# Weight operand buffers begun 16 to 128 bytes further, or hi and lo matmuls in another order, one variant for each MLP quarter

## The chip, the cores and the metric

The kernel runs on one core of one Trainium2 chip. The metric is the time of one execution in microseconds (us) of device time; lower is better. Times are given as the median of several runs. A profile comes from one further execution, whose instructions are recorded one by one.

## What is computed

A two-layer encoder trunk on 256 tokens of width 2048, in float32. Each layer mixes tokens with three groups of attention heads, and then runs an MLP whose hidden width is 8192. Cut to what the change touches:

```python
for l in range(DEPTH):                                   # DEPTH = 2
    ...                                                  # projections, attention, w_out
    u = jnp.square(jax.nn.relu(_rms(x, ln2_g[l]) @ w_ff1[l]))   # (256, 2048) @ (2048, 8192)
    x = x + u @ w_ff2[l]                                        # (256, 8192) @ (8192, 2048)
return _rms(x, ln_f_g)
```

## The kernel before

**Work as a row of units.** Every weight matrix is cut into units of at most 128 x 2048 values, which are listed in one order by hand (`layer_units`). The kernel walks this list. For unit i it writes the matmuls of TensorE, then the loads and splits of later units, then the evacuation of the unit's result. All five engines follow the written order; semaphores alone decide when each instruction may start.

**From a unit to operands.** SyncE's queue loads a unit into one of three `raw` buffers (L132). `split_to` then cuts it into chunks of 1024 columns. ScalarE rounds a chunk into a `hi` buffer (L147), VectorE subtracts and writes the rest into a `lo` buffer (L148). `hi` and `lo` have five buffers each, of 1024 values (4096 bytes) in a partition. Together they hold a float32 weight in two parts of type fp32r. Activations are kept in the same way, with the high part in columns 0 to 255 of a tile and the low part in columns 256 to 511 (`hx` for the inputs of a layer half, `ring` for others).

**The MLP.** In each layer it runs in four quarters of the hidden width. In each quarter 16 units named f come first and 16 named g after them. Quarter (l, q) below is quarter q of layer l, both counted from 0.

- An f unit makes 128 hidden columns. `mm_tile` runs over 16 k-tiles. For each it writes two matmuls into one PSUM bank, `acc`. The first, "h" here, has the hi weight tile (128 x 128) standing in the array and streams the 512 columns of `hx` (high and low part). The second, "l" here, has the lo weight tile standing and streams only the 256 columns of the high part into columns 256 to 511 of the bank. The two rows L297 and L298 of the profile are h and l. The first f unit of a layer has its own copy of this loop (L904, L905), with work between the k-tiles.
- A g unit multiplies back. In `v_mm` the activations stand in the array and the weights stream, 512 columns in each matmul: three matmuls (L616 to L618) for each k-tile and half of the tokens.

Each matmul has a weight load of its own (LDWEIGHTS, engine PEld in the profile), which the compiled program places ahead of it.

**The ring of small tiles.** `t1k` hands out tiles `t` of 128 x 256 from six buffers. The evacuation of an f unit takes two: one for the copied second half (L252), one for the sum (L253), which is then squared and split (L915 to L918). The first projections of a layer hold up to four `t` tiles, which GpSimd squares (L200 to L204).

**Addresses.** In the program as built, every `hi` and `lo` buffer, every `hx` tile and every `ring` tile begins on a multiple of 64 bytes in its partition. `hi`, `lo` buffers lie 4096 bytes apart before the change.

Of the kernel before, what the change touches and what calls it, by code (L numbers as in the profile page):

```python
# [10 lines left out]
F32 = mybir.dt.float32  # L11
F32R = mybir.dt.float32r
# [5 lines left out]
P = 128  # L18
T = 256
# [5 lines left out]
HL_BUFS = 5  # L25
# [14 lines left out]
def layer_units():  # L40
    names = [f"s{c}" for c in range(4)] + [f"a{m}" for m in range(4, 8)]
    names += ["b0", "b1", "un", "b2", "b3", "ur", "b4", "b5", "uk", "b6", "b7", "uv"]
    names += [f"v{k}" for k in range(8)]
    names += [f"c{m}" for m in range(12)]
    names += [f"o{m}" for m in range(10)]
    names += [f"w{m}" for m in range(6)]
    names += [f"p{m}" for m in range(8)]
    for q in range(4):
        names += [f"f{16 * q + m}" for m in range(16)]
        names += [f"g{16 * q + m}" for m in range(16)]  # L50
    cols = {"ur": 1024, "o": 1024, "w": 1024}
    return [(n, cols.get(n, cols.get(n[0], 2048))) for n in names]


UNITS = layer_units()
POS = {n: i for i, (n, _) in enumerate(UNITS)}


@with_exitstack
def kernel(  # L60
# [11 lines left out]
    pe, act, dve, pool, sp = nc.tensor, nc.scalar, nc.vector, nc.gpsimd, nc.sync  # L72
# [3 lines left out]
    sb = ctx.enter_context(tc.tile_pool(name="sb", bufs=1))  # L76
# [4 lines left out]
    def nm(s):  # L81
        uid[0] += 1
        return f"{s}_{uid[0]}"
# [5 lines left out]
        return sb.tile([P, 512], F32R, tag="hx", name=nm("hx"), bufs=16)  # L89

    def t1k():
        return sb.tile([P, T], F32, tag="t", name=nm("t"), bufs=6)

    def z2():
        return sb.tile([P, 512], F32, tag="z2", name=nm("z2"), bufs=4)
# [4 lines left out]
    def accbank():  # L100
        return ps.tile([P, 512], F32, tag="acc", name=nm("acc"), bufs=4)
# [3 lines left out]

    units = [(l,) + u for l in range(DEPTH) for u in UNITS]
    chunks = []
# [26 lines left out]
    def load_to(u):  # L134
        while loaded[0] < min(u, len(units)):
            load_part(loaded[0], 0, unit_src[loaded[0]][2])
            loaded[0] += 1

    def split_to(c):
        while splitted[0] < min(c, len(chunks)):  # L140
            k = splitted[0]
            u, o, n = chunks[k]
            load_to(u + 1)
            t = raw_t[u][:, o:o + n]
            hi = sb.tile([P, 1024], F32R, tag="hi", name=nm("hi"), bufs=HL_BUFS)
            lo = sb.tile([P, 1024], F32R, tag="lo", name=nm("lo"), bufs=HL_BUFS)
            act.activation(out=hi[:, :n], in_=t, func=AF.Copy)  # L147
            dve.tensor_tensor(out=lo[:, :n], in0=t, in1=hi[:, :n].bitcast(F32), op=ALU.subtract)  # L148
            hi_t[k], lo_t[k] = hi, lo
            splitted[0] += 1  # L150
            if k == unit_chunks[u][-1]:
                load_to(u + 1 + RAW_BUFS)
# [97 lines left out]
    def zevac(acc, dst):  # L250
        t = t1k()
        act.activation(out=t, in_=acc[:, T:], func=AF.Copy)  # L252
        dve.tensor_tensor(out=dst, in0=acc[:, :T], in1=t, op=ALU.add)  # L253
# [30 lines left out]
    def wtile(i, t, w=P):  # L284
        o = t * w
        for c in unit_chunks[i]:
            n = chunks[c][2]
            if o < n:
                return hi_t[c][:, o:o + w], lo_t[c][:, o:o + w]
            o -= n  # L290

    def mm_tile(i, t0, srcs, acc):
        n = len(srcs)
        for k in range(n):
            h, lo = wtile(i, t0 + k)
            s = srcs[k]
            pe.matmul(acc, h, s, start=k == 0, stop=False)  # L297
            pe.matmul(acc[:, T:], lo, s[:, :T], start=False, stop=k == n - 1)  # L298

    def layer(l):  # L300
# [3 lines left out]
        def at(name, pos, f, d=0):  # L304
            i = POS[name] if isinstance(name, str) else name
            sched[base + i + d, pos].append(f)

        def define(name, f, e):
            slot_pe[base + POS[name]], slot_ev[base + POS[name]] = f, e

# [35 lines left out]
        def gemm_acc(name, t0, srcs, acc=None):  # L346
            if acc is None:
                acc = accbank()
            mm_tile(base + POS[name], t0, srcs, acc)
            return acc  # L350
# [4 lines left out]
        def a_ev(m, acc):  # L355
            st["z", m] = t1k()
            zevac(acc, st["z", m])
# [31 lines left out]
        def mk_s(c):  # L389
            def f():  # L390
                if c == 0:
                    st["accs"] = [accbank() for _ in range(4)]
                for k in range(4):
                    s = hx[4 * c + k]
                    for m in range(4):
                        h, lo = wtile(base + POS[f"s{c}"], 4 * k + m)
                        a = st["accs"][m]
# [51 lines left out]
        def kpe():  # L449
            z, ta = st["kr"], st["ta"]  # L450
            k = ring(F32R)
            t1, t2 = t1k(), t1k()
            pool.tensor_tensor(out=t1[64:128], in0=z[64:128], in1=ta[64:128, 0:T], op=ALU.mult)
            dve.tensor_tensor(out=t2[64:96], in0=z[96:128], in1=ta[96:128, T:], op=ALU.mult)
            dve.tensor_tensor(out=t2[96:128], in0=z[64:96], in1=ta[64:96, T:], op=ALU.mult)
            dve.tensor_tensor(out=t1[64:128], in0=t1[64:128], in1=t2[64:128], op=ALU.add)
            dve.tensor_tensor(out=t1[64:128], in0=t1[64:128], in1=st["r1b"][64:128], op=ALU.mult)
            dve.tensor_copy(out=t1[0:64], in_=t1[64:128])
            act.activation(out=k[:, :T], in_=t1, func=AF.Copy)
            dve.tensor_tensor(out=k[:, T:], in0=t1, in1=k[:, :T].bitcast(F32), op=ALU.subtract)  # L460
            st["kpe"] = k
# [145 lines left out]
        def v_mm(name, srcs, k0, kt, accs=None, n=4):  # L607
            for k in range(n):
                h, lo = wtile(base + POS[name], k, 512)
                s = srcs[k0 + k]  # L610
# [82 lines left out]
        def c_rope(h):  # L693
            z = st["zc"]
            t2 = z2()
            for eng, d, s in ((dve if h == 5 else pool, 0, 64), (pool, 64, 0)):
                eng.tensor_tensor(out=t2[d:d + 64], in0=z[s:s + 64], in1=st["sc"][s:s + 64], op=ALU.mult)  # L697
            pool.tensor_tensor(out=z, in0=z, in1=st["cc"], op=ALU.mult)
            st["crr"] = z, t2
# [9 lines left out]
        for h in range(6):  # L709
            at(POS["c0"] + 2 * h + 2, "pre" if h == 5 else "mid", lambda h=h: c_rope(h))  # L710
            at(POS["c0"] + 2 * h + 2, "post", c_rope2)
# [292 lines left out]
    for m in range(8):  # L1004
        first_x(m)
        if m % 2:
            split_to((m + 1) // 2 + 1)
# [8 lines left out]
    for i in range(nslots):  # L1016
        slot_pe[i]()
        run(i, "pre")
        target = unit_chunks[i][0] + HL_BUFS + (2 if i == 0 else 0)
        if i + 1 < nslots:  # L1020
            target = max(target, unit_chunks[i + 1][-1] + 1)
        split_to(min(target, splitted[0] + 1))
        run(i, "mid")
        split_to(target)
        run(i, "post")
        slot_ev[i]()
        run(i, "ext")
# [47 lines left out]
def _weights(inp):  # L1075
# [15 lines left out]
    for l in range(DEPTH):  # L1091
# [8 lines left out]
        uv = np.concatenate([wukv[:, h * 256 + 128:h * 256 + 256] for h in range(4)], axis=1)  # L1100
        for name, n in UNITS:
            kind = name[0]
# [77 lines left out]
```

## Time and profile before

| what | value |
|---|---|
| median of 3 runs | 2190.47 us |
| lowest and highest run | 2187.46 and 2190.63 us |
| time of the profiled execution | 2186.54 us |
| span of its profile, first to last instruction | 2184.8 us |
| mean granted TensorE clock | 0.996 |
| instructions in the profile | 27949 |

The span leaves out 1.7 us of the profiled execution's time that lie before its first and after its last instruction. A row of a timeline begins with the start and the duration of an instruction. TensorE's matmuls overlap, so a matmul's duration is longer than the time until the next one starts; the spacing of starts is what a matmul costs. "PEclk" is the granted share of the clock.

### The profile page before, as it was taken

How to read it: one execution, taken by the hardware profiler on the slowest of the kernel's cores; microseconds unless marked ns; L12 is line 12 of the kernel's file. 1: busy time of each engine (PE TensorE's matmuls, PEld its weight loads, DVE VectorE, ACT ScalarE, POOL GpSimd, SP SyncE). 2: the span in 40 equal slices, each digit the busy share in tenths (PEclk: the TensorE clock that was granted, in tenths of full speed). 3: DMA queues.
4: the chain of work that ended last, by engine and by line, in shares of the span. 5: the costliest groups of instructions: out<-in, count | busy, mean ns of one | idle time of the engine just before them, and what ended most of it. 6: DMA issues, size and time to landing. Idle time of an engine off the chain costs nothing.

```text
span 2184.8 us, 27949 instructions
## 1 busy us (share of the span) xinstructions
PE 2150.8 (98%) x11132; PEld 1828.6 (84%) x11132; DVE 1383.4 (63%) x1795; ACT 1028.6 (47%) x1517; POOL 299.1 (14%) x250
## 2 busy tenths in 40 slices
PE   9999999999999999999999999999999999999997
PEld 8878878888888888888888888788888888888886
DVE  6886865665564565566578878656646655655654
ACT  6445545543443444344454555554434434444443
POOL 2643630000000000000027346200000000000000
PEclk9999999999999999999999999999999999999999
DMA  8444354555555555555554443545655555565563
GB/s 300 164 146 153 116 192 174 175 210 193 174 189 205 177 182 201 182 193 177 208 184 145 163 138 132 180 169 193 205 194 171 202 190 176 193 205 179 178 228 116
DMA packets 60179, 396.14 MB, mean 181 GB/s; under 512 B 6800, under 2 KB 6800, under 8 KB 15376
## 3 DMA queue, kind: packets, MB, share of 16 engines
q1 hardware_dynamic: 57600, 388.52, 51.7%
q10 hardware_dynamic: 2448, 5.83, 0.8%
q8 instruction: 87, 1.43, 0.3%
q14 instruction: 44, 0.36, 0.0%
HBM read 392.23 MB, written 2.10 MB: 180 GB/s over the span
## 4 chain that ended last, share of the span: by engine, by line
PE 47%; issue 39%; DVE 7%; POOL 3%; ACT 3%; DMA 1%; SPq 0%; POOLq 0%; DVEq 0%; ACTq 0%
PE acc L297 12%; PE acc L616 8%; PE acc L617 7%; PE acc L618 7%; PE acc L298 6%; DVE lo L148 3%; ACT hi L147 1%; PE acc L398 1%; DMA raw<-in_w_dram 1%; POOL z L332 1%; POOL z L697 1%; PE acc L399 1%; PE att L297 1%; DVE z L337 1%; PE att L715 0%
## 5 line engine op out<-in xcount | busy, mean ns | idle before, releaser
L148 DVE TENSOR_TENSOR lo<-raw,hi 128x1024 fp32r<-128x1024 f32 (+1 forms) x735 | 909.2, 1263 | 401.5 <-ACT hi L147 398.5
L297 PE MATMUL acc<-hx,hi 128*128 128x512 f32 x2720 | 963.5, 399 | 2.2 <-ACT hi L147 2.2
L147 ACT ACTIVATE hi<-raw 128x1024 fp32r<-128x1024 f32 (+1 forms) x735 | 752.1, 1051 | 384.2 <-PE acc L618 348.7
L298 PE MATMUL acc<-hx,lo 128*128 128x256 f32 x2720 | 765.2, 281 | 2.8 <-DVE lo L148 2.8
L297 PEld LDWEIGHTS acc<-hx,hi 128*128 128x128 f32 x2720 | 512.8, 189 | 126.6 <-ACT hi L147 2.9
L298 PEld LDWEIGHTS acc<-hx,lo 128*128 128x128 f32 x2720 | 515.7, 190 | 3.6 <-DVE lo L148 3.4
L616 PE MATMUL acc<-hi,ring 128*128 128x512 f32 x1296 | 506.6, 391 | 0.0
L617 PE MATMUL acc<-lo,ring 128*128 128x512 f32 x1296 | 505.2, 390 | 0.0
L618 PE MATMUL acc<-hi,ring 128*128 128x512 f32 x1296 | 505.2, 390 | 0.0
L618 PEld LDWEIGHTS acc<-hi,ring 128*128 128x128 f32 x1296 | 243.4, 188 | 50.7
L616 PEld LDWEIGHTS acc<-hi,ring 128*128 128x128 f32 x1296 | 243.5, 188 | 50.0
L617 PEld LDWEIGHTS acc<-lo,ring 128*128 128x128 f32 x1296 | 243.5, 188 | 49.2
L252 ACT ACTIVATE t<-acc 128x256 f32<-128x256 f32 x192 | 72.5, 381 | 310.7 <-PE acc L298 303.4
L253 DVE TENSOR_TENSOR t<-acc,t 128x256 f32<-128x256 f32 x140 | 59.0, 424 | 136.2 <-ACT t L252 136.1
L222 POOL TENSOR_TENSOR st<-st,nhalf 128x2 f32<-128x2 f32 x9 | 10.0, 1116 | 791.8 <-DVE st L221 791.8
L200 POOL TENSOR_TENSOR sacc<-t 128x256 f32<-128x256 f32 x4 | 3.4, 841 | 833.7 <-DVE t L253 833.7
L917 ACT ACTIVATE ring<-t 128x256 fp32r<-128x256 f32 x128 | 53.5, 418 | 125.9 <-DVE t L915 125.9
L946 DVE SCALAR_TENSOR_TENSOR xt<-acc,st,xt 128x512 f32<-128x512 f32 x64 | 45.8, 751 | 86.2 <-PE acc L618 86.2
L918 DVE TENSOR_TENSOR ring<-t,ring 128x256 fp32r<-128x256 f32 x128 | 54.5, 425 | 62.7 <-ACT ring L917 62.7
L257 ACT ACTIVATE sq<-xt 128x512 f32<-128x512 f32 x40 | 25.1, 628 | 72.3 <-DVE xt L946 44.0
L915 DVE SCALAR_TENSOR_TENSOR t<-t 128x256 f32<-128x256 f32 x128 | 54.4, 425 | 4.4
L332 POOL TENSOR_TENSOR z<-z,ring 32x512 f32<-32x512 f32 x30 | 52.9, 1763 | 21.7 <-DVE z L253 20.2
(157 smaller groups left out, 1549.9 us busy)
## 6 DMA issues: line engine op xcount, KB each, us to landing
raw<-in_w_dram SPq DMA_DIRECT2D x347, 1024.0 KB, 4.9
raw<-in_w_dram SPq DMA_DIRECT2D x39, 512.0 KB, 3.7
ring<-in_xfeat_dram SPq DMA_DIRECT2D x8, 256.0 KB, 7.6
ring<-in_tabs_dram ACTq DMA_DIRECT2D x8, 256.0 KB, 3.3
xt<-in_xtok_dram ACTq DMA_DIRECT2D x2, 1024.0 KB, 9.2
ring<-in_gfin_dram ACTq DMA_DIRECT2D x4, 256.0 KB, 3.9
out_dram<-xt SPq DMA_DIRECT2D x2, 512.0 KB, 4.1
raw<-in_w_dram SPq DMA_DIRECT2D x2, 256.0 KB, 4.0
```

The source lines that it names most:

```text
L147: act.activation(out=hi[:, :n], in_=t, func=AF.Copy)
L148: dve.tensor_tensor(out=lo[:, :n], in0=t, in1=hi[:, :n].bitcast(F32), op=ALU.subtract)
L252: act.activation(out=t, in_=acc[:, T:], func=AF.Copy)
L253: dve.tensor_tensor(out=dst, in0=acc[:, :T], in1=t, op=ALU.add)
L297: pe.matmul(acc, h, s, start=k == 0, stop=False)
L298: pe.matmul(acc[:, T:], lo, s[:, :T], start=False, stop=k == n - 1)
L332: eng.tensor_tensor(out=v2[d:d + 32], in0=zc[s:s + 32], in1=s_[s:s + 32], op=ALU.mult)
L616: pe.matmul(a, sh, h, start=first, stop=False)
L617: pe.matmul(a, sh, lo, start=False, stop=False)
L618: pe.matmul(a, sl, h, start=False, stop=last)
L915: dve.scalar_tensor_tensor(out=z, in0=z, scalar=0.0, in1=z, op0=ALU.max, op1=ALU.mult)
L918: dve.tensor_tensor(out=d[:, T:], in0=z, in1=d[:, :T].bitcast(F32), op=ALU.subtract)
```

## The change

Three things are changed.

- Quarters (0, 1), (0, 2), (0, 3) and (1, 0): the chunk begins 4, 8, 16 or 32 values (16, 32, 64 or 128 bytes) behind the start of its `hi` and `lo` buffer. This holds for the f units and the g units of the quarter.
- Quarters (1, 1), (1, 2) and (1, 3): the f units write their matmuls in blocks, "hhll", "hllh" and eight h followed by eight l. The g units keep their order.
- Each `hi` and `lo` buffer is 1056 values long (4224 bytes, so the buffers lie 4224 bytes apart in every part of the kernel), and `t` has five buffers for six.

Quarter (0, 0), the first unit of (1, 0)'s own loop and everything outside the MLP keep their order of instructions. In quarter (1, 0) the first f unit's chunks are shifted too.

```diff
+SHIFT = {(0, 1): 4, (0, 2): 8, (0, 3): 16, (1, 0): 32}
+BLOCK = {(1, 1): "hhll", (1, 2): "hllh", (1, 3): "hhhhhhhhllllllll"}
...
-        return sb.tile([P, T], F32, tag="t", name=nm("t"), bufs=6)
+        return sb.tile([P, T], F32, tag="t", name=nm("t"), bufs=5)
...
+    def quarter_of(unit):
+        return (unit[0], int(unit[1][1:]) // 16) if unit[1][0] in "fg" else None
+
+    def shift_of(unit):
+        return SHIFT.get(quarter_of(unit), 0)
...
-            hi = sb.tile([P, 1024], F32R, tag="hi", name=nm("hi"), bufs=HL_BUFS)
-            lo = sb.tile([P, 1024], F32R, tag="lo", name=nm("lo"), bufs=HL_BUFS)
+            sh = shift_of(units[u])
+            hi = sb.tile([P, 1024 + 32], F32R, tag="hi", name=nm("hi"), bufs=HL_BUFS)[:, sh:sh + 1024]
+            lo = sb.tile([P, 1024 + 32], F32R, tag="lo", name=nm("lo"), bufs=HL_BUFS)[:, sh:sh + 1024]
...
     def mm_tile(i, t0, srcs, acc):
         n = len(srcs)
+        block = BLOCK.get(quarter_of(units[i]))
+        if block:
+            half = len(block) // 2
+            for k0 in range(0, n, half):
+                ks = {"h": iter(range(k0, k0 + half)), "l": iter(range(k0, k0 + half))}
+                for j, c in enumerate(block):
+                    k = next(ks[c])
+                    w = wtile(i, t0 + k)
+                    s = srcs[k]
+                    last = k0 + half == n and j == len(block) - 1
+                    if c == "h":
+                        pe.matmul(acc, w[0], s, start=k == 0, stop=last)
+                    else:
+                        pe.matmul(acc[:, T:], w[1], s[:, :T], start=False, stop=last)
+            return
         for k in range(n):
```

On TensorE's queue the first f unit of quarter (1, 1) reads as follows before the change. In a row, the tile behind "<-" with hx is what streams, the one with hi or lo is the weight tile; the numbers behind names tell buffers apart.

```order
L297 MATMUL acc_2759_14318<-hx_2450_12548,hi_2752_14278 128x512
L298 MATMUL acc_2759_14318<-hx_2450_12548,lo_2753_14279 128x256
L297 MATMUL acc_2759_14318<-hx_2451_12551,hi_2752_14278 128x512
L298 MATMUL acc_2759_14318<-hx_2451_12551,lo_2753_14279 128x256
L297 MATMUL acc_2759_14318<-hx_2452_12554,hi_2752_14278 128x512
L298 MATMUL acc_2759_14318<-hx_2452_12554,lo_2753_14279 128x256
```

The same place of TensorE's queue after the change:

```order
L314 MATMUL acc_2759_14318<-hx_2450_12548,hi_2752_14278 128x512
L314 MATMUL acc_2759_14318<-hx_2451_12551,hi_2752_14278 128x512
L316 MATMUL acc_2759_14318<-hx_2450_12548,lo_2753_14279 128x256
L316 MATMUL acc_2759_14318<-hx_2451_12551,lo_2753_14279 128x256
L314 MATMUL acc_2759_14318<-hx_2452_12554,hi_2752_14278 128x512
L314 MATMUL acc_2759_14318<-hx_2453_12557,hi_2752_14278 128x512
```

The second h has moved ahead of the first l; in each four matmuls there is now one step from h to h, one from h to l, one from l to l and one from l to h. Quarter (1, 2), "hllh", has the same four steps, begun at another point.

The first f unit of quarter (1, 3), from its fifth h on, after the change (before it, h and l alternate as above):

```order
L314 MATMUL acc_3223_17070<-hx_2467_12652,hi_3216_17030 128x512
L314 MATMUL acc_3223_17070<-hx_2468_12655,hi_3216_17030 128x512
L314 MATMUL acc_3223_17070<-hx_2469_12658,hi_3216_17030 128x512
L314 MATMUL acc_3223_17070<-hx_2470_12661,hi_3216_17030 128x512
L316 MATMUL acc_3223_17070<-hx_2450_12548,lo_3217_17031 128x256
L316 MATMUL acc_3223_17070<-hx_2451_12551,lo_3217_17031 128x256
L316 MATMUL acc_3223_17070<-hx_2452_12554,lo_3217_17031 128x256
L316 MATMUL acc_3223_17070<-hx_2453_12557,lo_3217_17031 128x256
```

All eight h of a chunk now stand ahead of its first l, so that the lo buffer is first read seven h later in the order than before.

## Rows read from the trace of the kernel before

**Rows 1.** The page: busy time of each engine, share of the span, instructions.

```profile
PE 2150.8 (98%) x11132; PEld 1828.6 (84%) x11132; DVE 1383.4 (63%) x1795; ACT 1028.6 (47%) x1517; POOL 299.1 (14%) x250
```

**Rows 2.** Busy time by stretch: f and g of (0,0), (0,1); then (1,0), (1,1).

```profile
core 0: us, PE busy (x) PEld busy (x) DVE busy (x) ACT busy (x) POOL busy (x), PEclk, DMA share, GB/s
386.96:470.16 83.20, 83.20 (x483) 72.75 (x481) 57.01 (x80) 41.27 (x61) 0.00 (x0) 1.00 0.56 191
470.16:557.21 87.05, 87.05 (x387) 72.12 (x385) 44.56 (x42) 35.49 (x35) 0.00 (x0) 1.00 0.59 204
557.21:647.65 90.44, 90.44 (x514) 78.47 (x512) 57.78 (x79) 41.56 (x61) 0.00 (x0) 1.00 0.51 176
647.65:734.71 87.06, 87.06 (x386) 72.13 (x385) 44.55 (x42) 35.49 (x35) 0.00 (x0) 1.00 0.58 204
...
1468.92:1553.72 84.80, 84.80 (x483) 73.63 (x482) 57.05 (x80) 41.24 (x61) 0.00 (x0) 1.00 0.56 188
1553.72:1640.77 87.05, 87.05 (x387) 72.12 (x386) 44.55 (x42) 35.49 (x35) 0.00 (x0) 1.00 0.59 204
1640.77:1731.20 90.43, 90.43 (x513) 78.54 (x512) 57.78 (x79) 41.56 (x61) 0.00 (x0) 1.00 0.53 176
```

**Rows 3.** What TensorE waited for, 380 to 1003 us.

```profile
PE acc L904 <- DVE hx L192: 0.8, 2, 0.4
```

**Rows 4.** Timeline of TensorE's matmuls inside f of quarter (0, 1).

```profile
600.18 0.28 PE L298 MATMUL acc<-hx,lo 128*128 128x256 f32 x1
600.30 0.40 PE L297 MATMUL acc<-hx,hi 128*128 128x512 f32 x1
600.54 0.28 PE L298 MATMUL acc<-hx,lo 128*128 128x256 f32 x1
600.66 0.40 PE L297 MATMUL acc<-hx,hi 128*128 128x512 f32 x1
600.89 0.28 PE L298 MATMUL acc<-hx,lo 128*128 128x256 f32 x1
601.01 0.39 PE L297 MATMUL acc<-hx,hi 128*128 128x512 f32 x1
601.24 0.28 PE L298 MATMUL acc<-hx,lo 128*128 128x256 f32 x1
```

**Rows 5.** Timeline of weight loads (PEld), same place.

```profile
600.30 0.19 PEld L298 LDWEIGHTS acc<-hx,lo 128*128 128x128 f32 x1
600.54 0.19 PEld L297 LDWEIGHTS acc<-hx,hi 128*128 128x128 f32 x1
```

**Rows 6.** Timeline of TensorE where f of quarter (0, 1) ends and g begins.

```profile
647.53 0.28 PE L298 MATMUL acc<-hx,lo 128*128 128x256 f32 x1
647.65 0.40 PE L616 MATMUL acc<-hi,ring 128*128 128x512 f32 x1
647.88 0.40 PE L617 MATMUL acc<-lo,ring 128*128 128x512 f32 x1
648.12 0.39 PE L618 MATMUL acc<-hi,ring 128*128 128x512 f32 x1
...
649.26 0.39 PE L617 MATMUL acc<-lo,ring 128*128 128x512 f32 x1
```

**Rows 7.** Timeline of TensorE in attention: 256-column matmuls in a row.

```profile
216.40 0.28 PE L298 MATMUL acc<-hx,lo 128*128 128x256 f32 x1
216.51 0.28 PE L715 MATMUL att<-pt,ring 128*128 128x256 f32 x1
...
216.99 0.28 PE L716 MATMUL att<-pt,ring 128*128 128x256 f32 x1
```

**Rows 8.** Timelines of VectorE and ScalarE: one f unit's evacuation.

```profile
602.62 0.38 ACT L252 ACTIVATE t<-acc 128x256 f32<-128x256 f32 x1 [1.94 <-PE acc L298]
604.46 0.43 DVE L918 TENSOR_TENSOR ring<-t,ring 128x256 fp32r<-128x256 f32 x1 [0.54 <-ACT ring L917]
```

**Rows 9.** Timelines of GpSimd and VectorE, first projections of layer 0.

```profile
37.46 1.59 POOL L203 TENSOR_TENSOR sq<-t 64x256 f32<-64x256 f32 x1
42.21 0.42 DVE L253 TENSOR_TENSOR t<-att,t 128x256 f32<-128x256 f32 x1 [0.90 <-ACT t L252]
```

## The prediction

> **What bounds the kernel now.** I read the page first: TensorE (PE) is busy for 2150.8 of 2184.8 us, VectorE for 1383.4, ScalarE for 1028.6 [rows 1]. A busy matmul engine can hide waits, so I read the waits of TensorE next, over the MLP of layer 0: 0.8 us in all, both at the first f unit [rows 3]. The same view over the MLP of layer 1 answers with the same line. So inside the quarters that are changed TensorE waits for no other engine, and its clock is granted in full (PEclk 1.00, which is 2.4 GHz) in every one of the stretches [rows 2]. Nothing that VectorE, ScalarE or a DMA does there sets the time. What is left is how close one matmul's start follows the last one's.
>
> For that I cut the MLP into stretches from the first matmul of a kind to the first of the next kind [rows 2]. A g stretch holds 16 units of 24 matmuls, 384 in all, and takes 87.05 us: 226.7 ns for a 512-column matmul. Six of the seven g stretches up to (1, 2) lie between 87.05 and 87.07 us; the one of (0, 3) is broken by the end of the layer. A full f stretch holds 256 pairs of h and l and takes 90.44 us: **353.3 ns a pair**. All six of (0, 1) to (0, 3) and (1, 1) to (1, 3) read 90.43 or 90.44. The stretch of (0, 0) has 240 pairs, since its first unit has its own loop, and takes 83.20 us: **346.7 ns a pair**. The stretch of (1, 0) has 240 pairs too and takes 84.80: 353.3 again. The code of these two is the same. So one and the same string of matmuls has two steady speeds, 6.7 ns apart, and stays in the one that it falls into for a whole stretch.
>
> The timeline shows the slow one as a pattern of three pairs that takes 1.06 us: steps from h to l of 0.24, 0.23, 0.23 us, steps from l to h of 0.12 each [rows 4]. The pattern of three runs through the boundaries of units, though a unit has 16 pairs, a chunk eight and the weight buffers turn over every five chunks. So it is not tied to which tile is read. A weight load starts together with the matmul ahead of its own, at 600.30 and 600.54 [rows 4, 5]: it lies beneath that matmul. That 0.19 us long load stands under an l of 0.12 us, so its row holds time that does not block the next matmul.
>
> **The change, part by part.**
>
> *Shorter ring of t tiles.* An f unit takes two tiles, and the last reader of the second ends 2.27 us after the first was begun (602.62 to 604.89) [rows 8]. With five buffers a tile comes back after two units at the earliest, 2 x 16 x 353 ns = 11.3 us. In the first projections VectorE's first sum after the four held tiles, at 42.21, must now also wait for GpSimd to have read an old tile; the last of those reads ends at 39.05 [rows 9], 3.1 us earlier. Cost 0. Were this cover gone, VectorE would be late by what is missing and with it the lo splits queued behind that sum; those are for matmuls several us later.
>
> *Longer buffers, 4224 bytes apart.* Every chunk still begins on a multiple of 64 bytes. The tiles of before lie at many multiples of 512 bytes from one another and g reads 226.7 ns whichever is read. Cost 0.
>
> *Chunks begun 16 to 128 bytes further.* No instruction is added. The writers, L147 and L148, have slack: ScalarE is busy for 41.56 and VectorE for 57.78 of 90.44 us [rows 2]. What the reader, TensorE, does with an operand that begins 16 or 32 bytes behind a multiple of 64, this trace does not show. From below: if the start decided which of the two speeds f falls into, the three full stretches would gain 256 x 6.7 ns = 1.7 us each and (1, 0) 1.6: 6.7 us. From above: one such step of 6.7 ns on each f pair and each g matmul of the two quarters that leave multiples of 64: (256 + 384) x 6.7 ns = 4.3 us a quarter, 8.5 us in all; if all four paid, 17 us. I take 0, because (0, 0) and (1, 0) differ in speed with the same buffers, and the pattern ignores which tile is read; that puts the cause in timing and not in addresses.
>
> *Matmuls in blocks.* Four steps have to be priced.
> - h to h: 226.7 ns from a steady g stretch. Just behind a change from l, it is slower: 0.23, then 0.24 us; seven such steps from 647.65 to 649.26 take 1.61 us in place of 1.587 [rows 6].
> - l to l: four steps from 216.51 to 216.99 take 0.48 us, 0.12 each [rows 7].
> - h to l: 0.70 us in three, 0.233. l to h: 0.12 [rows 4].
>
> "hhll" and "hllh" have one of each in two pairs: 0.2267 + 0.2333 + 0.12 + 0.12 = 0.700 us, for 0.7067 before. That is 6.7 ns in 128 groups of a quarter, **0.85 us a quarter**. From below: both pairs at the fast speed, 0.6933, is 1.7 us a quarter. From above: the h to h step always at 0.24 and the h to l step too, 0.72, would lose 13 ns a group, 1.7 us a quarter.
>
> Eight h and eight l: 1.61 + 0.233 + 7 x 0.12 + 0.12 = 2.803 us for 8 x 0.3533 = 2.827 before, 24 ns in 32 groups: **0.8 us**. Below: the fast speed, 1.7 us gained. Above: l to l steps of 0.125, 0.3 us lost.
>
> The order changes waits too. The first l of eight stands behind seven more h, 7 x 0.227 = 1.6 us later than before, and what fills the lo buffer has that much more room. A hi buffer is free earlier, by seven l that stood between its h, 0.8 us. No wait is added on TensorE.
>
> Sum: 0.85 + 0.85 + 0.8 = **2.5 us gained**, with bounds of 5.1 gained and 3.7 lost from the order, and of 6.7 gained and 8.5 lost from the starts. Against its own time of 2186.54 us the profiled execution would come to 2184.0. That execution lies 3.9 us under the median of the runs and 0.9 under the lowest. The mean of all four executions is 2188.8, which gives 2186.3; the median gives 2188.0. I take **2187 us**.
>
> A measurement of this kernel tells about 0.2%, 4.4 us, from no change: the runs alone spread over 3.2 us.
>
> *A rule against it.* The rows give 226.7 ns for 512 columns and 353.3 for 512 and 256 together, whatever stands there [rows 2]. The Trainium skill (TensorE: Matmul & The Clock Gate, section Back-to-back issue gap) prices a warm matmul by its own columns alone, N / 2.4 + 2.5 ns, so a pair would be 325 ns in any order, by an estimate from that page, and a block would gain nothing. The trace disagrees with its size (353.3) and, by the two speeds of one string, with a price that neighbours do not touch.
>
> **The rivals.**
>
> *Each matmul has a fixed price.* Then blocks cost the same as pairs, the sum is 0, and the time stays between 2186.5 and 2190.5 us. For it: seven of eight f stretches run at one speed. Against it: (0, 0) does not. By the page's rule above this is what would happen. Chance 0.2.
>
> *The fast speed throughout.* The extra 6.7 ns come where two streams into TensorE meet at a bad phase: the weight load and the moving columns start within the same 10 ns [rows 4, 5]. A shifted start or a block would break the lock. Blocks at the fast speed gain 5.1 us; shifted quarters at the fast speed up to 6.7 more. With the blocks alone 2189 - 5 = 2184, with both 2177. For it: the fast speed exists, in (0, 0). Against: the phase seems to be one of time. Chance 0.17.
>
> *Slower: starts off 64 bytes cost a step.* If TensorE reads in pieces of 64 bytes, a tile that begins 16 or 32 bytes further takes one piece more. The price is the 8.5 us above, in (0, 1) and (0, 2): 2189 + 8.5 - 2.5 = 2195. It decides the sign as soon as a step costs over 2 ns a matmul in these two quarters (2.5 us over 1280 steps). For it: nothing in the trace has such a start. Against it: no row. The Trainium skill (SBUF — State Buffer, section Door 1: The DMA port swizzle) names lines of 16 bytes; all four shifts keep that, and no run here shows it. Chance 0.13.
>
> **How the numbers follow.** The forecast has 0.5. Its own range is 2183 to 2191. The range that should hold 8 in 10 takes in the fast rival with blocks alone and most of the slow one: **2180 to 2194**. Faster by over 0.2%: most of the fast rival and a tail of the forecast, 0.19. Slower by over 0.2%: the slow rival and a little of the others' spread, 0.13. Within 0.2%: 0.68.
>
> **What would show it.** In the profile after, the f stretches of (1, 1) and (1, 2) should take 89.6 us, and so should that of (1, 3), with h to h steps of 0.227 to 0.235 and l to l steps of 0.12. The stretches of (0, 1) to (0, 3) should stay at 90.44 and all g stretches at 87.05. The stretch of (0, 0) may fall to either speed, 83.20 or 84.80, since it is set by how it starts. Block stretches at 88.75 would speak for the fast rival, 90.44 for fixed prices. A g stretch above 87.1 in (0, 1) or (0, 2) would be the slow rival's mark, and shifted f stretches that differ from (0, 3) with the same g would say that addresses do matter. I would be wrong if a row of l is slower than the 0.12 that four attention matmuls show, or if a lasting wait of TensorE turns up in a quarter.

## The result and the profile after

The changed kernel takes **2202.52 us**, the median of 4 runs from 2199.75 to 2205.37; the kernel before takes 2188.97, the median of 4 runs from 2186.63 to 2190.63. The ratio is 1.0063, with a 95% interval of 1.0045 to 1.008. The change is slower by about 13.5 us, where 2187 and no measurable difference had been forecast, and it lies 8.5 us above the top of the predicted range.

The page of the kernel after, engine by engine, answers to [rows 1]:

```profile
span 2198.0 us, 27960 instructions
...
PE 2164.4 (98%) x11132; PEld 1830.0 (83%) x11132; DVE 1381.4 (63%) x1795; ACT 1029.2 (47%) x1517; POOL 298.3 (14%) x250
```

TensorE runs as many matmuls as before and is busy 13.6 us longer, while the span has grown by 13.2 us; VectorE and ScalarE do the same work. The chain of causes therefore stays inside TensorE. Its waits over the MLP of layer 0 confirm it; the one row is that of [rows 3], so nothing new is waited for:

```profile
PE acc L928 <- DVE hx L201: 0.8, 2, 0.4
```

Next come the windows of the kernel after, cut as in [rows 2]: f and g of (0, 0), (0, 1) and (0, 2), f of (0, 3); then f and g of (1, 0), (1, 1) and (1, 2), f of (1, 3).

```profile
387.64:471.40 83.76, 83.76 (x483) 73.51 (x481) 56.99 (x80) 41.29 (x61) 0.00 (x0) 1.00 0.56 190
471.40:560.33 88.93, 88.93 (x386) 72.08 (x385) 44.61 (x42) 35.47 (x35) 0.00 (x0) 1.00 0.56 200
560.33:649.86 89.53, 89.53 (x513) 78.35 (x512) 57.78 (x79) 41.60 (x61) 0.00 (x0) 1.00 0.52 178
649.86:738.23 88.37, 88.37 (x386) 72.04 (x385) 44.60 (x42) 35.46 (x35) 0.00 (x0) 1.00 0.57 201
738.23:827.65 89.42, 89.42 (x514) 78.17 (x513) 57.78 (x79) 41.70 (x61) 0.00 (x0) 1.00 0.52 178
827.65:916.97 89.32, 89.32 (x386) 72.09 (x385) 44.60 (x42) 35.51 (x35) 0.00 (x0) 1.00 0.57 200
916.97:1006.77 89.80, 89.80 (x513) 78.74 (x512) 57.77 (x79) 41.62 (x61) 0.00 (x0) 1.00 0.52 177
1477.47:1561.42 83.95, 83.95 (x482) 73.57 (x481) 56.99 (x80) 41.29 (x61) 0.00 (x0) 1.00 0.56 190
1561.42:1650.10 88.68, 88.68 (x387) 72.07 (x385) 44.60 (x42) 35.47 (x35) 0.00 (x0) 1.00 0.58 201
1650.10:1739.94 89.84, 89.84 (x513) 78.58 (x512) 57.78 (x79) 41.58 (x61) 0.00 (x0) 1.00 0.53 177
1739.94:1828.91 88.97, 88.97 (x386) 72.09 (x385) 44.60 (x42) 35.47 (x35) 0.00 (x0) 1.00 0.59 200
1828.91:1918.75 89.84, 89.84 (x513) 78.06 (x512) 57.78 (x79) 41.58 (x61) 0.00 (x0) 1.00 0.53 177
1918.75:2007.69 88.94, 88.94 (x385) 72.08 (x384) 44.62 (x42) 35.47 (x35) 0.00 (x0) 1.00 0.57 200
2007.69:2097.50 89.81, 89.81 (x513) 78.68 (x512) 57.79 (x79) 41.59 (x61) 0.00 (x0) 1.00 0.52 177
```

The clock is 1.00 in each. Read the g stretches first, the lines of 384 matmuls: 87.05 before, and now 88.37 to 89.32. The first of them belongs to quarter (0, 0), which has neither a shift nor a block; it has lost 1.9 us. Together the six g stretches lose 10.8 us. The full f stretches go the other way, from 90.44 to between 89.4 and 89.8; all eight f stretches together give 4.7 us back.

The rest of the loss is outside these fourteen stretches. The windows of the kernel after by stage are: up to the first f unit's own loop; the MLP of layer 0 up to its last g; that g and the first projections of layer 1; the rest of layer 1 up to its MLP; this MLP up to its last g; the end.

```profile
0.00:383.85 383.85, 372.07 (x1999) 316.67 (x1999) 277.80 (x408) 206.19 (x367) 149.12 (x129) 0.99 0.51 177
383.85:1006.77 622.92, 622.10 (x3183) 526.87 (x3182) 366.02 (x444) 275.30 (x354) 0.00 (x0) 1.00 0.54 188
1006.77:1104.49 97.72, 97.72 (x451) 80.26 (x449) 52.90 (x57) 45.82 (x65) 0.00 (x0) 1.00 0.53 185
1104.49:1473.67 369.18, 360.32 (x1946) 307.26 (x1944) 269.50 (x390) 189.40 (x331) 148.52 (x120) 0.99 0.47 160
1473.67:2097.50 623.83, 623.00 (x3183) 527.03 (x3181) 366.05 (x444) 275.11 (x354) 0.00 (x0) 1.00 0.55 188
2097.50:2198.00 100.50, 89.16 (x386) 71.90 (x384) 49.12 (x52) 37.36 (x49) 0.70 (x1) 0.96 0.47 167
```

The same stages of the kernel before took 383.17, 619.49, 96.18, 366.28, 621.10 and 98.58 us. The differences are 0.7, 3.4, 1.5, 2.9, 2.7 and 1.9, in sum 13.2. Attention and projections are touched by one part of the change alone, the distance of the buffers (the ring of `t` apart), and they read longer too; how much of that is the change is taken up at the end of the section on the prediction.

Inside a g stretch the timeline of the kernel after shows what has moved:

```profile
516.51 0.40 PE L640 MATMUL acc<-hi,ring 128*128 128x512 f32 x1
516.75 0.40 PE L641 MATMUL acc<-lo,ring 128*128 128x512 f32 x1
516.98 0.39 PE L642 MATMUL acc<-hi,ring 128*128 128x512 f32 x1
517.21 0.40 PE L640 MATMUL acc<-hi,ring 128*128 128x512 f32 x1
```

Three steps take 0.70 us, where three steady ones took 0.68 (3 x 226.7 ns from [rows 2]). A g matmul now costs 88.93 / 384 = 231.6 ns. There is no gap in which TensorE waits; every matmul follows the last one a little later.

### The profile page after: what moved, and what is told of

It reads as the page before. It is cut to its first block, busy times and chain, and to the rows that moved or that the text cites. A ratio compares the mean times of both kernels' runs of the same rounds, so it can differ in the third digit from the quotient of the medians.

```text
span 2198.0 us, 27960 instructions
## 1 busy us (share of the span) xinstructions
PE 2164.4 (98%) x11132; PEld 1830.0 (83%) x11132; DVE 1381.4 (63%) x1795; ACT 1029.2 (47%) x1517; POOL 298.3 (14%) x250
## 4 chain that ended last, share of the span: by engine, by line
PE 45%; issue 39%; DVE 7%; ACT 3%; POOL 3%; DMA 2%; SPq 0%; ACTq 0%; POOLq 0%; DVEq 0%
PE acc L321 12%; PE acc L640 8%; PE acc L641 8%; PE acc L642 8%; PE acc L322 6%; DVE lo L157 3%; ACT hi L156 1%; POOL z L356 1%; DMA raw<-in_w_dram 1%; POOL z L721 1%; PE acc L422 1%; DVE z L361 1%; DMA xt<-in_xtok_dram 1%; PE att L740 0%; PE att L739 0%
## 5 line engine op out<-in xcount | busy, mean ns | idle before, releaser
L321 PE MATMUL acc<-hx,hi 128*128 128x512 f32 x1952 | 686.8, 395 | 2.7 <-ACT hi L156 2.7
L322 PE MATMUL acc<-hx,lo 128*128 128x256 f32 x1952 | 549.2, 281 | 2.8 <-DVE lo L157 2.8
L640 PE MATMUL acc<-hi,ring 128*128 128x512 f32 x1296 | 514.2, 397 | 0.0
L642 PE MATMUL acc<-hi,ring 128*128 128x512 f32 x1296 | 509.1, 393 | 0.0
L321 PEld LDWEIGHTS acc<-hx,hi 128*128 128x128 f32 x1952 | 367.6, 188 | 86.5 <-ACT hi L156 3.4
L322 PEld LDWEIGHTS acc<-hx,lo 128*128 128x128 f32 x1952 | 368.0, 189 | 3.5 <-DVE lo L157 3.4
L314 PE MATMUL acc<-hx,hi 128*128 128x512 f32 x768 | 225.6, 395 | 0.0
L316 PEld LDWEIGHTS acc<-hx,lo 128*128 128x128 f32 x768 | 131.2, 188 | 25.8
L316 PE MATMUL acc<-hx,lo 128*128 128x256 f32 x768 | 137.6, 281 | 0.0
L314 PEld LDWEIGHTS acc<-hx,hi 128*128 128x128 f32 x768 | 124.3, 188 | 8.6
L970 DVE SCALAR_TENSOR_TENSOR xt<-acc,st,xt 128x512 f32<-128x512 f32 x64 | 46.3, 751 | 89.8 <-PE acc L642 89.8
```

Of the source, the lines that this page charges most:

```text
L314: pe.matmul(acc, w[0], s, start=k == 0, stop=last)
L316: pe.matmul(acc[:, T:], w[1], s[:, :T], start=False, stop=last)
L640: pe.matmul(a, sh, h, start=first, stop=False)
L642: pe.matmul(a, sl, h, start=False, stop=last)
```

## The experiments

Every ratio is to the kernel before, run on the same chip, with its 95% interval. "Place" below is where a tile begins in its partition, as the built program says. In the kernel before all `hi`, `lo`, `hx` and `ring` tiles begin at 192 modulo 256. At 4224 bytes apart the five `hi` buffers alternate between 192 and 64, and each `lo` buffer has the place that its `hi` has not. "Nearer" and "further" below count modulo 256: a tile begun 496 bytes further is called 16 bytes nearer.

**The buffers alone.** Both tables of the change are emptied; the longer buffers and five `t` stay.

```diff
-SHIFT = {(0, 1): 4, (0, 2): 8, (0, 3): 16, (1, 0): 32}
-BLOCK = {(1, 1): "hhll", (1, 2): "hllh", (1, 3): "hhhhhhhhllllllll"}
+SHIFT = {}
+BLOCK = {}
```

> The changed kernel's buffers alone: hi and lo 4224 bytes apart and five t tiles, no shifted start, every f unit in the old order. Theory A, the distance: in a g unit the streams follow one another as hi, lo, hi, and with 4224 bytes between buffers the lo buffer of a chunk begins 128 bytes off the hi buffer's place in a row of 512 bytes; each such step costs TensorE some 4 to 6 ns. Then all of the loss is here: 2200 to 2205 us, every g stretch at 88.4 to 89.4 us, every f stretch at 89.3 to 89.9. Theory B, the start: chunks begun 16 or 32 bytes behind a multiple of 64 cost a step. Then this kernel is within 2 us of the kernel before, 2187 to 2191, with g at 87.05.

Measured: 2200.44 us, 1.0041 (1.0026 to 1.0056). Its span of 2197.7 us is that of the whole change to 0.3 us, in one execution of each; by the medians it loses 10.1 us where the whole change loses 13.5, and the intervals of the two ratios overlap. The windows of g of (0, 0) and f of (0, 1):

```profile
472.73:561.66 88.93, 88.93 (x387) 72.08 (x385) 44.61 (x42) 35.50 (x35) 0.00 (x0) 1.00 0.56 200
561.66:650.93 89.27, 89.27 (x513) 78.41 (x512) 57.78 (x79) 41.62 (x61) 0.00 (x0) 1.00 0.52 178
```

All six g stretches read 88.93 to 88.99, and all six full f stretches 89.23 to 89.39. The part that had been costed at nothing carries most of the loss.

**The blocks alone**, with the buffers 4096 bytes apart as before, and five `t`.

```diff
+SHIFT = {}
...
-            hi = sb.tile([P, 1024 + 32], F32R, tag="hi", name=nm("hi"), bufs=HL_BUFS)[:, sh:sh + 1024]
-            lo = sb.tile([P, 1024 + 32], F32R, tag="lo", name=nm("lo"), bufs=HL_BUFS)[:, sh:sh + 1024]
+            hi = sb.tile([P, 1024], F32R, tag="hi", name=nm("hi"), bufs=HL_BUFS)[:, sh:sh + 1024]
+            lo = sb.tile([P, 1024], F32R, tag="lo", name=nm("lo"), bufs=HL_BUFS)[:, sh:sh + 1024]
```

> The blocks alone, with buffers 4096 bytes apart again (five t tiles stay). Theories A and B both: all g stretches at 87.05 us, f of (0,1) to (0,3) at 90.44, and no loss. What it measures is the price of the order without the other changes: f of (1,1) to (1,3) at 88.7 to 89.8 us if a block spares the slow speed, 90.44 if each matmul has a fixed price; in all 0 to 5 us faster than before.

Measured: 2186.3 us, 0.9979 (0.9969 to 0.9988). The windows of f in (0, 0) and in the three block quarters:

```profile
385.02:469.82 84.80, 84.80 (x482) 73.53 (x481) 57.05 (x80) 41.31 (x61) 0.00 (x0) 1.00 0.54 187
...
1642.14:1731.31 89.17, 89.17 (x514) 77.81 (x513) 57.80 (x79) 41.60 (x61) 0.00 (x0) 1.00 0.52 178
1818.36:1907.53 89.17, 89.17 (x514) 77.81 (x513) 57.83 (x79) 41.66 (x61) 0.00 (x0) 1.00 0.52 179
1994.57:2083.93 89.36, 89.36 (x513) 78.65 (x512) 57.79 (x79) 41.59 (x61) 0.00 (x0) 1.00 0.52 178
```

The blocks gain 1.27, 1.27 and 1.08 us, 3.6 in all, against 90.44. In the profiled run (0, 0), which has no block, fell to 353.3 ns a pair and gave 1.6 of it back. Five `t` cost nothing to be seen.

**The shifts alone**, with chunks 4096 bytes apart: `hi` and `lo` are each cut out of one long tile. At the turns between quarters, where the shift grows or falls back to 0, a chunk's write covers the first or last 4 to 32 columns of a neighbouring chunk, so this kernel's arithmetic differs in those few weight columns. TensorE's waits over the MLP of layer 0 stay at 0.8 us.

```diff
+SHIFT = {(0, 1): 4, (0, 2): 8, (0, 3): 16, (1, 0): 32}
+BLOCK = {}
...
+                big.append(sb.tile([P, HL_BUFS * 1024 + 128], F32R, tag="hi", name="hi", bufs=1))
+                big.append(sb.tile([P, HL_BUFS * 1024 + 32], F32R, tag="lo", name="lo", bufs=1))
+            sh += k % HL_BUFS * 1024
+            hi = big[0][:, sh:sh + 1024]
+            lo = big[1][:, sh:sh + 1024]
```

> The four shifted starts alone: hi chunks lie in one long tile, 4096 bytes apart, lo chunks too, and the two tiles are at the same place in a row of 512 bytes; each quarter's chunks begin 16, 32, 64 or 128 bytes further as in the change. Theory A: g stays at 87.05 us in every quarter, since within a quarter all streams are shifted alike; total within 5 us of before. Theory B: g of (0,1) and (0,2) at 88.5 us or more. A third theory C, that the place of the stream against the place of the standing operand's tile counts: g of all four shifted quarters changes, by 1 to 2 us each, and that of (0,0) and (1,1) to (1,3) does not.

Measured: 2194.07 us, 1.0018 (1.0008 to 1.0027). The windows of g of (0, 0), f and g of (0, 1) and (0, 2), then g of (1, 0), f and g of (1, 1):

```profile
470.16:557.21 87.05, 87.05 (x386) 72.08 (x385) 44.54 (x42) 35.49 (x35) 0.00 (x0) 1.00 0.58 204
557.21:645.96 88.75, 88.75 (x514) 78.18 (x513) 57.77 (x79) 41.60 (x61) 0.00 (x0) 1.00 0.52 179
645.96:734.91 88.95, 88.95 (x386) 72.20 (x385) 44.59 (x42) 35.50 (x35) 0.00 (x0) 1.00 0.56 200
734.91:825.36 90.45, 90.45 (x514) 78.54 (x513) 57.79 (x79) 41.66 (x61) 0.00 (x0) 1.00 0.51 176
825.36:914.95 89.59, 89.59 (x386) 71.97 (x385) 44.63 (x42) 35.53 (x35) 0.00 (x0) 1.00 0.56 199
...
1559.01:1648.25 89.24, 89.24 (x387) 72.36 (x385) 44.61 (x42) 35.48 (x35) 0.00 (x0) 1.00 0.58 199
1648.25:1737.00 88.75, 88.75 (x513) 78.25 (x512) 57.75 (x79) 41.61 (x61) 0.00 (x0) 1.00 0.53 179
1737.00:1824.09 87.09, 87.09 (x387) 72.08 (x386) 44.55 (x42) 35.49 (x35) 0.00 (x0) 1.00 0.59 204
```

Now the loss in g follows the shift, quarter by quarter: 1.9 us for 16 bytes, 2.5 for 32, 2.2 for 128, and none in the quarters without one. For 64 bytes, in (0, 3), the first 120 g matmuls take 27.47 us for 27.24 before, 1.9 ns each. So it is the place that costs, and not some property of the longer buffers. That 128 bytes costs as much as 16 rules out the 64-byte rival. In this kernel `hi` and `lo` move together against `ring`. The f stretch of (1, 1) is neither shifted nor reordered and has its operands at their old place modulo 256, yet it runs at 346.7 ns a pair (88.75 / 256) and not at the 353.3 of before: f has both speeds at one and the same place.

**`lo` moved and `hi` not**, by 128 unused bytes between the two sets of buffers; then by 256. The tiles that lie behind `lo` move along; among them are small operands of attention, but nothing else that TensorE reads in the f and g stretches below.

```diff
             hi = sb.tile([P, 1024], F32R, tag="hi", name=nm("hi"), bufs=HL_BUFS)
+            if k == 0:
+                sb.tile([P, 32], F32, tag="padlo", name="padlo", bufs=1)
             lo = sb.tile([P, 1024], F32R, tag="lo", name=nm("lo"), bufs=HL_BUFS)
```

> The kernel before with 128 unused bytes between the five hi and the five lo buffers: buffers of one kind stay 4096 bytes apart, but each lo lies 128 bytes off its hi in a row of 512. Theory A: as slow as the 4224 bytes, g at 88.4 to 89.4 us in every quarter, f at 89.3 to 89.9, total 2199 to 2206. If instead the turn from one chunk's buffer to the next counts, g stays at 87.05 and the total at 2187 to 2191.

Measured with 128 bytes: 2200.11 us, 1.0039 (1.0024 to 1.0054). Nothing is shifted, lengthened or reordered here, and the time is that of the buffers alone. The windows of g of (0, 0) and f of (0, 1):

```profile
473.18:561.92 88.74, 88.74 (x386) 72.17 (x385) 44.55 (x42) 35.48 (x35) 0.00 (x0) 1.00 0.57 201
561.92:651.52 89.60, 89.60 (x513) 78.29 (x512) 57.76 (x79) 41.65 (x61) 0.00 (x0) 1.00 0.51 177
```

The kernel with 256 bytes has 64 in place of 32.

> As the run with 128 unused bytes between the hi and the lo buffers, with 256 bytes. Theory A, the step from hi to lo: the step is there, twice as long, so g at 88.4 us or more and a total of 2197 to 2206. Theory C in rows of 256 bytes: lo against the ring tiles is at the same place as hi, so g at 87.05 in every quarter and the total within 4 us of before.

Measured: 2191.46 us, 1.0003 (0.9994 to 1.0012). Its g of (0, 1):

```profile
650.29:737.36 87.07, 87.07 (x386) 72.11 (x385) 44.54 (x42) 35.49 (x35) 0.00 (x0) 1.00 0.58 204
```

A distance of 256 bytes is as good as none, one of 128 is not.

**`hi` and `lo` both moved by 256**, with the unused bytes ahead of `hi`.

```diff
+            if k == 0:
+                sb.tile([P, 64], F32, tag="padhi", name="padhi", bufs=1)
             hi = sb.tile([P, 1024], F32R, tag="hi", name=nm("hi"), bufs=HL_BUFS)
```

> 256 unused bytes ahead of the hi buffers, so that hi and lo are both 256 bytes further and no step is between them. Theory A and theory C in rows of 256: g at 87.05, total within 4 us of before. If the row is 512 bytes long and the place against the ring tiles counts: g at 88 to 90 us, total 2196 or more.

Measured: 2191.68 us, 1.0006 (0.9996 to 1.0016), with g at 87.05 to 87.07. Counting in 512 bytes would have shown here; it does not.

**A long pitch that is a multiple of 256.** The test of the account as a rule: `hi` buffers longer than those of the change, 4352 = 17 x 256 bytes apart.

```diff
-            hi = sb.tile([P, 1024], F32R, tag="hi", name=nm("hi"), bufs=HL_BUFS)
+            hi = sb.tile([P, 1024 + 64], F32R, tag="hi", name=nm("hi"), bufs=HL_BUFS)[:, :1024]
...
-        return sb.tile([P, T], F32, tag="t", name=nm("t"), bufs=6)
+        return sb.tile([P, T], F32, tag="t", name=nm("t"), bufs=5)
```

> The kernel before with hi buffers 4352 bytes apart (17 rows of 256) and five t tiles: longer buffers, as in the change, but every buffer at the same place in a row of 256. Theory C: g at 87.05 to 87.10 and f at 90.44 in the full quarters, total 2186 to 2193, no loss to before. If longer buffers cost by themselves, or rows are 512 bytes long: g above 88, total above 2196.

Measured: 2189.76 us, 1.0003 (0.9994 to 1.0012). Its g of (0, 0) and f of (0, 1):

```profile
470.69:557.76 87.07, 87.07 (x386) 72.11 (x385) 44.55 (x42) 35.49 (x35) 0.00 (x0) 1.00 0.57 204
557.76:648.20 90.44, 90.44 (x513) 78.47 (x512) 57.77 (x79) 41.59 (x61) 0.00 (x0) 1.00 0.52 176
```

Longer buffers and five `t` cost nothing when every tile keeps its place modulo 256.

**The operand of f moved instead.** `hx` is cut out of one long tile, at places 16 bytes nearer (o = 124 + ...) or 16 bytes further (o = 4 + ...); the weights keep their place modulo 256.

```diff
-        return sb.tile([P, 512], F32R, tag="hx", name=nm("hx"), bufs=16)
+        if not bighx:
+            bighx.append(sb.tile([P, 16 * 512 + 128], F32R, tag="hx", name="hx", bufs=1))
+        nhx[0] += 1
+        o = 124 + (nhx[0] - 1) % 16 * 512
+        return bighx[0][:, o:o + 512]
```

> Order and weight buffers as before the change; only the sixteen hx tiles begin 496 bytes further, which is 16 bytes ahead of the weight buffers in a row of 512. In every f unit a weight tile then begins 16 bytes behind the hx tile that streams, as in quarter (0,1) of the run with shifted starts alone, where f took 88.74 us; g, which does not read hx, keeps its places. Theory C, the place of what streams against the place of what is loaded, counted in a row of 256 bytes: every f stretch at 88.7 to 88.8 us (83.2 for the 240 pairs of a layer's first quarter), g at 87.05, and some loss outside the MLP where hx is the standing operand; 2177 to 2184 us in all. If the speed that f falls into is an accident of how a stretch begins: f stays at 90.44 in most quarters and the total at 2187 to 2191.

Measured, 16 nearer: 2191.64 us, 1.0005 (0.9995 to 1.0014); f stays at 90.43 and g at 87.05. Theory C had f at 88.7 to 88.8 here and missed.

> The same with hx 16 bytes further in place of 16 bytes back. If the sign of the distance does not count, f at 88.7 to 88.8 us again. If it counts, f between 88.7 and 90.4 us; g at 87.05 either way. Total 2178 to 2192.

Measured, 16 further: 2185.69 us, 0.9977 (0.9967 to 0.9987). The windows of f of (0, 0), g of (0, 0) and f of (0, 1):

```profile
388.71:475.10 86.39, 86.39 (x483) 74.63 (x481) 57.05 (x80) 41.26 (x61) 0.00 (x0) 1.00 0.54 185
475.10:562.19 87.09, 87.09 (x387) 72.07 (x385) 44.54 (x42) 35.49 (x35) 0.00 (x0) 1.00 0.58 204
562.19:650.95 88.76, 88.76 (x514) 79.21 (x512) 57.74 (x79) 41.57 (x61) 0.00 (x0) 1.00 0.52 179
```

All six full f stretches run at 346.7 ns a pair (88.76 / 256). The first quarters of both layers fall to a third speed, 360 ns (86.39 / 240), and g does not move. So 16 bytes are no cost in themselves: `hx` moved forward helps the full f stretches, moved backward it does nothing, and in g 16 bytes hurt.

**The weights 16 bytes nearer**, which gives f the same distance as the run above and g a distance that it did not have before; `hi` and `lo` move together, in long tiles, with five `t`.

```diff
+                big.append(sb.tile([P, HL_BUFS * 1024 + 128], F32R, tag="hi", name="hi", bufs=1))
+                big.append(sb.tile([P, HL_BUFS * 1024 + 128], F32R, tag="lo", name="lo", bufs=1))
+            sh = 124 + k % HL_BUFS * 1024
+            hi = big[0][:, sh:sh + 1024]
+            lo = big[1][:, sh:sh + 1024]
```

> hx at its old place and all hi and lo chunks 16 bytes nearer, so that f has the same distance as in the faster run, and the distance in g is 16 bytes beyond a row of 256 (with shifted starts alone it was 16 bytes short of one, and g took 88.96). Theory C: f at 88.76 in the full quarters, 90.2 in the first of a layer; g changes in every quarter, 88 to 90 us if each distance but 0 costs g, below 87.05 if g gains on this side as f does. Theory A, steps between successive streams: no step is added, so g at 87.05.

Measured: 2209.05 us, 1.0092 (1.0075 to 1.011). The windows of g of (0, 0) and f of (0, 1):

```profile
470.61:561.49 90.88, 90.88 (x387) 73.29 (x386) 44.63 (x42) 35.48 (x35) 0.00 (x0) 1.00 0.55 196
561.49:650.25 88.76, 88.76 (x514) 78.08 (x513) 57.76 (x79) 41.61 (x61) 0.00 (x0) 1.00 0.51 179
```

All six full f stretches run at 346.7 again, now with `hx` where it always was: at this distance it does not matter which operand was moved. The first quarters do not follow the distance. They take 83.21 and 84.78 us (346.7 and 353.3 ns a pair) where theory C expected the 360 ns of the run above. And g has its highest price, 90.88 / 384 = 236.7 ns, though every `hi` and `lo` streams from one place modulo 256. So streams that differ among themselves are not needed for the loss; a place other than that of the standing `ring` tile is enough.

In g only the streamed tile was ever moved. The runs with `hx` moved hold the other case: in attention, stretches of 24 matmuls stream `hi` and `lo` past a standing `hx`. One such stretch before, then with `hx` 16 bytes further:

```profile
160.03:165.49 5.46, 5.46 (x27) 4.51 (x25) 4.60 (x8) 3.67 (x8) 0.87 (x2) 1.00 0.30 84
159.63:165.22 5.59, 5.59 (x26) 4.54 (x25) 4.59 (x8) 3.68 (x8) 0.87 (x2) 1.00 0.36 94
```

The streamed tiles kept their place, and a matmul went from 227.5 to 232.9 ns (5.59 / 24). So the loss is not bound to the place of the streamed tile by itself. With `hx` 16 bytes nearer the same stretch takes 5.47 us, next to no loss, though the streamed tile is then 16 bytes further than the standing one, which cost g 4.9 ns a matmul. So the distance by itself does not fix the price either.

**Better kernels.** `hx` 16 bytes further, with blocks in six quarters; then with "hhll" only in the first quarter of each layer, against the third speed.

```diff
+BLOCK = {(0, 0): "hhll", (0, 1): "hhll", (0, 2): "hllh", (0, 3): "hhhhhhhhllllllll", (1, 0): "hllh", (1, 1): "hhhhllll"}
...
+        o = 4 + (nhx[0] - 1) % 16 * 512
```

> hx 16 bytes further, as in the run that was faster, and blocks in six quarters: hhll in (0,0), (0,1), hllh in (0,2), (1,0), eight and eight in (0,3), hhhhllll in (1,1); (1,2) and (1,3) in the old order. Theory C: g at 87.09 throughout and f of (1,2), (1,3) at 88.76. If a block saves what it saved at the old place (1.1 to 1.3 us a quarter from 90.44), f of the block quarters would be 87.5 to 87.7; if 88.75 is a floor for 256 pairs at any order, 88.7 to 89.4. In (0,0) and (1,0), where the run before this fell to 360 ns a pair (90.2 us), a block should come out at 86 to 87.5 us. Total 2176 to 2186.

Measured: 2181.25 us, 0.9966 (0.9954 to 0.9979). Its full block stretches take 89.14 to 89.17 us, its plain ones 88.76: at this place a block costs 0.4 us in a full quarter. In (0, 0) and (1, 0) it gains, with 83.62 us for the 86.39 of (0, 0) in the run without blocks.

```diff
+BLOCK = {(0, 0): "hhll", (1, 0): "hhll"}
```

> The version that the runs point to: hx 16 bytes further, hhll in the first quarter of each layer alone, the old order elsewhere. Theory C: f of (0,0) and (1,0) at 87.4 us with their first unit, the six full f stretches at 88.76, g at 87.05 to 87.10. That is 1.6 us less than the run with blocks in six quarters: 2178 to 2181 us, ratio to before 0.995 to 0.997.

Measured: 2179.13 us, 0.9962 (0.995 to 0.9975), faster than both kernels of this case. Its six full f stretches take 88.76 us, and its f of (0, 0):

```profile
386.23:469.84 83.61, 83.61 (x482) 73.41 (x481) 56.97 (x80) 41.32 (x61) 0.00 (x0) 1.00 0.55 190
```

Its lead over the kernel with six block quarters is within their intervals.

## Why the prediction was wrong

- **The step that failed is "Longer buffers, 4224 bytes apart … Cost 0".** Alone it takes the span to 2197.7 us, 12.9 of the 13.2 us lost; by the medians it is 10.1 of 13.5. Its reason was that tiles at many multiples of 512 bytes from one another all read 226.7 ns. In the built program that holds for `hi`, `lo` and `hx`, while the `ring` tiles that stand in g lie an odd multiple of 256 bytes from them; either way it showed only that multiples of 256 are free. 4224 is 16 x 256 + 128. Before choosing 0, the places of the new buffers should have been set beside places that the trace holds; with no operand of f or g off a multiple of 256, the trace of before gave no price, and the term needed bounds in every stretch that reads a weight.
- **"That puts the cause in timing and not in addresses"** was half wrong. The pattern of three pairs could not show a price of place, since all tiles had one place modulo 256, and moving one operand by 16 bytes put all six full f stretches at 346.7 ns. But f also has two speeds at one place, in (0, 0) and (1, 0) before and in (0, 0) and (1, 1) of the shifts alone. Both count.
- **Chunks begun further: taken as 0.** At the 4096-byte distance they cost 1.9 to 2.5 us of g in each of the three quarters with 16, 32 and 128 bytes, which the bound of 4.3 a quarter held. On top of the 4224-byte distance they add little, since `hi` and `lo` already stand in two places there: g of (0, 1) to (1, 0) reads 88.37 to 89.32 with shifts, 88.93 to 88.99 without.
- **Matmuls in blocks: right in sign, too small, and only in part by the terms of the sum.** At 4096 bytes the gain is 3.6 us for 2.5 forecast, within its bounds: 1.27 a quarter for 0.85 with "hhll" and "hllh", 1.08 for 0.8 with eight and eight. The timeline of (1, 1) in the run with the blocks alone, where x2 joins two matmuls in one row:

```profile
1699.96 0.63 PE L314 MATMUL acc<-hx,hi 128*128 128x512 f32 x2
1700.42 0.39 PE L316 MATMUL acc<-hx,lo 128*128 128x256 f32 x2
1700.65 0.63 PE L314 MATMUL acc<-hx,hi 128*128 128x512 f32 x2
```

  The second h starts 0.23 us behind the first (0.63 less the 0.40 of one matmul). Over the quarter the mean steps are 232.9 ns from h to h, 233.3 from h to l, 114.6 from l to l and 115.9 from l to h. The sum had 226.7, 233.3, 120 and 120. The cheap step from h to h, on which the gain had been built, did not come; the steps from l were cheaper than priced. That the gain came out near the forecast is in part luck. At 4224 bytes it is a loss: 89.84, 89.84 and 89.81, where the plain order there reads 89.28, 89.39 and 89.27. A price of steps taken from one place did not hold in another.
- **The ring of five `t`: 0**, as forecast.
- **The slow rival** had the right sign and the right mark, a g stretch above 87.1 us. Its mechanism was wrong: it tied the price to starts off 64 bytes in two quarters, and the loss stands in every quarter. Its time of 2195 was too low for that reason. **Fixed prices** fall with both kinds of stretch. **The fast speed throughout** exists, in the six full f stretches of the last kernel above, but not by what the change does.
- **The range** was too narrow because a cost of the whole kernel, one price for every matmul that streams or holds a weight, had been bounded in two quarters only.

What the runs show is a dependence on where the two operands begin; what they do not show is why. That an odd place costs by itself is shown where `hi` and `lo` move together. Whether a change of place from one stream to the next costs on top is open: with `lo` alone moved by 128 bytes, one matmul of three, three matmuls lose 3 x (88.74 - 87.05) / 384 = 13 ns, and with all three moved by 128 they lose 17, so the loss is not shared out by what moved. Open too are which start of an f stretch leads to which speed, and why 16 bytes backward did nothing to f when `hx` moved, while the one quarter with that same distance from shifted weights ran at 88.75; since f has that speed at the old place too, one quarter decides nothing.

Not all of the 13.2 us in the span is shown to come from the change. The rest of layer 1 up to its MLP (attention and projections) reads 2.9 us more after it, but this stage also reads more in the runs that keep every place modulo 256, as with the pitch of 4352 bytes:

```profile
1099.39:1467.43 368.04, 359.15 (x1946) 307.01 (x1944) 269.36 (x390) 189.39 (x331) 148.50 (x120) 0.99 0.47 161
```

That is 1.8 us over the 366.28 of before; with the blocks alone and the two moves by 256 it is 1.6, 2.5 and 1.6. So most of the 2.9 us is not shown to come from the change, and the 0.7 us of the first stage is less than its spread in these four runs (381.2 to 385.2 us). The 6.1 us of the two MLP stages and the 3.4 us of the stages with their last g stretches are seen in f and g. In the last kernel the f stretches give about 10.8 us and the span 8.4 (2184.8 to 2176.4); the difference lies mostly in the same stage, which reads 3.0 us more than before.

## What to carry to other kernels

When a matmul stream has no waits and still does not run at one spacing, look at where its two operands begin, and keep them at one place modulo 256 bytes unless a run shows another to be better, as 16 bytes did for f here. A pad, a longer buffer or a tile placed ahead of others moves every later tile; before costing it at nothing, ask whether the new place occurs anywhere in the trace. Compare the stretches that a change does not mean to touch first: here quarter (0, 0) pointed to the buffers in one row.

## What the runs showed of the hardware

- **TensorE's spacing depends on where the streamed and the standing tile begin.** 512 columns of g cost 226.7 ns with both at one place modulo 256 bytes; 231.6 with the streamed tile 16 bytes further, 233.3 at 32, 232.4 at 128, and 236.7 at 16 bytes nearer. With the standing tile moved instead, in attention, it was 232.9 at 16 bytes further and about 228 at 16 nearer. The Trainium skill (SBUF — State Buffer, section Operand start alignment) asks of a start only that it is a multiple of the element's size, and says of itself that this is about legality and that its runs timed nothing; the rows agree with the first half, since all these starts run, and add a price of up to 4.4%.
- **f in its old order has at least three steady speeds, 346.7, 353.3 and 360 ns a pair**, at a full clock. In the kernel before a stretch keeps the one in which it starts, and tiles at one place allow both of the first two. `hx` 16 bytes further than the weights brought all full stretches to the first, blocks to about 348.3 (89.17 / 256).
